# Splitting the last two gated tiles of a Conformer module by token halves, and adding up its layer-norm sums on other engines than TensorE

## The chip, the cores and the metric

The kernel runs on one core of a Trainium2 chip. A core has five engines that work at the same time, each through its own list of instructions in order: TensorE (PE, matrix products), VectorE (DVE), ScalarE (ACT), GpSimd (POOL), and SyncE (SP), whose list here holds nothing but DMA issues. The metric is the device time of one execution in microseconds (us), as the median of the runs shown. Times inside the program are us from the start of one profiled execution.

## The reference, cut to what matters

Two layers over 512 tokens and 1024 channels. Layer 0 is a hybrid of state-space heads and attention with a SwiGLU feed-forward; layer 1 is a Conformer convolution module with another SwiGLU; a final RMS norm closes. The change lies inside the Conformer module:

```python
def conformer_conv(h, w1, b1, w_dw, b_dw, ln_g, ln_b, w2, b2):
    a, gt = jnp.split(h @ w1 + b1, 2, axis=-1)      # first pointwise layer, 1024 -> 2 x 1024
    u = a * jax.nn.sigmoid(gt)                      # gate
    u = causal_depthwise_conv(u, w_dw, b_dw)        # 31 taps along the tokens, per channel
    u = jax.nn.silu(layer_norm(u, ln_g, ln_b))      # mean and variance over the 1024 channels
    return u @ w2 + b2                              # second pointwise layer
```

The norm needs all channels of a token before any of them goes on. The convolution is causal: an output token needs itself and the 30 tokens before it.

## The kernel before, in words

Channels lie on the 128 partitions and tokens along the free dimension, so the 1024 channels are 8 tiles, numbered k = 0 to 7, of 128 x 512. `CUTS` holds the two halves of the tokens, `H0` (0 to 255) and `H1` (256 to 511).

A product of exact 32-bit quality is made of three matmuls on rounded parts: weights and activations are split into a high part (`hi`, a cast on ACT, L208) and a low part (`lo`, a subtraction, L209, on DVE or POOL), and `products` (L212 to 225) adds hi*hi (L221), hi*lo (L222) and lo*hi (L224) over 8 contraction tiles: 24 matmuls an output tile. `slab` (L195) loads 1 MB of weights into one of two `raw` buffers by an SP DMA (L200), and fills one of two `whi` and one of two `wlo` buffers; each is free again when its last reader is done.

Stages of the Conformer module, for each k:

- **Products** `pa` and `pg` (`a` and the gate) for 512 tokens, 48 matmuls, into the two banks with the tag `pj`.
- **Gate**: sigmoid on ACT (L992), `u = (pa + b) * sigmoid` on DVE (L996) into `cu`, with zeros ahead of the first token.
- **Shifted copies** (`shifted`, L962): 16 SP DMAs (L967) copy `cu` into `u4[k]` (in the profile: `u`), which holds each group of 32 channels four times, shifted by 0 to 3 tokens, so that a matmul of 32 output channels covers four taps.
- **Convolution** (`conv`, L969): 32 matmuls (8 steps of 4 taps, times 4 channel groups, into `cps`, L975) with filters `w4[k]` that POOL builds (L930); ACT evicts each half into `cv[k, half]` (L979). The profile counts two instructions for one of these 32-bit matmuls; products with rounded parts count one.
- **Layer norm** (`layer_norm(c)`, L1006) by halves of the tokens: 8 matmuls with a matrix of 1/1024 (`mu`, L1011) give the mean on all partitions, DVE subtracts it (L1015), ACT squares (L1019), 16 matmuls against ones give the variance (`var`, L1021), DVE takes the inverse root in 12 small steps, two matmuls spread it (`lnr`, L288), DVE multiplies (L1028), ACT applies silu (L1029) and rounds to `ch` (L1030), and DVE makes the low part `cl` (L1031).
- **Second pointwise layer** (`pw2(c)`, L1035): 8 output tiles `pq` for H0, then 8 for H1; DVE adds each to the residual `xT` (L608), whose squares feed the next norm.

The code is written with the convolution of tile k-2 behind the products of tile k, the first halves of 4 to 7 ahead, `layer_norm(H0)`, the second halves of 4 to 7, `layer_norm(H1)`, and then `pw2`. The order on every engine is not this one: a scheduler lays the instructions out when the program is built, by its own estimates of durations, and waits go by data and by buffers. So the order that stands in the built program is shown below where it matters.

## Time and profile before

| | us |
|---|---|
| median of 3 runs (lowest, highest) | 1847.52 (1847.27, 1849.47) |
| the profiled execution's own time | 1844.22 |
| its span, first to last instruction | 1842.5 |
| TensorE busy in the span | 1764.2 (96%) |
| DVE, ACT, POOL busy | 999.3, 740.7, 347.6 |
| mean granted TensorE clock | 0.983 |

The profile page gives the busy time of each engine, its rows by source line, and the chain of work that ended last. A row such as `L975 PE MATMUL cps<-u,w 128*32 128x256 f32 x512 | 31.9, 380 | 1.6` reads: line 975, TensorE, output `cps` from `u` and `w`, shapes, 512 instructions; 31.9 us busy and 380 ns on average; 1.6 us idle just before them, with what ended that idle time. Matmuls overlap in the array, so the pitch from one start to the next is shorter than one duration. In views by stretches of time (windows), a row gives the stretch, its length, each engine's busy time with its instructions, the granted clock, the share of the DMA engines and GB/s. In a timeline, a row gives start, duration and a count of merged instructions, with idle time before them in brackets.

The Conformer module runs from about 1256 us, where the third product tile starts, to 1460 us, where the second feed-forward starts.

### The profile page before, as it was taken

Reading aid. Unit: us, or ns where it says so; the run is one execution under the profiler, and the core shown is the slowest. Engines: PE = TensorE matmul, PEld = TensorE weight load, DVE = VectorE, ACT = ScalarE, POOL = GpSimd, SP = SyncE. Lnnn points to the kernel's source line nnn. Section 1 sums busy time; section 2 is a strip of 40 time slices with the busy share of each in tenths; the row PEclk is TensorE's granted clock in tenths of the full one; section 3 lists DMA queues with packets and bytes.
Section 4 is the critical chain, followed back from the end, with each engine's and each line's share of the span. In section 5 each row is a group of like instructions: output and inputs, shape, how many; then the busy total and the mean of one; then the engine's idle time right before and its main releaser. Section 6 shows DMA issues by size and latency. Waiting matters only on the chain.

```text
span 1842.5 us, 25006 instructions
## 1 busy us (share of the span) xinstructions
PE 1764.2 (96%) x9775; PEld 1438.8 (78%) x9775; DVE 999.3 (54%) x1944; ACT 740.7 (40%) x1473; POOL 347.6 (19%) x278
## 2 busy tenths in 40 slices
PE   5999999999999999977999999999999999999998
PEld 3777687788778787767888888897568988888887
DVE  7756657555655556658674673373204743333336
ACT  6465646455454444434222222252215532122235
POOL 0013314224542423432000000021121100000001
PEclk9999999999999999988999999999998999999999
DMA  9455544454545445343655562253640522323233
GB/s 309 125 143 152 154 119 125 111 150 138 133 131 149 127 157 142 104 128 115 228 187 179 183 206 81 87 177 78 178 122 24 161 92 92 92 92 114 70 97 132
DMA packets 233219, 247.85 MB, mean 135 GB/s; under 512 B 14074, under 2 KB 198204, under 8 KB 233101
## 3 DMA queue, kind: packets, MB, share of 16 engines
q1 hardware_dynamic: 223117, 208.50, 38.0%
q0 software_dynamic: 9984, 37.75, 6.2%
q8 instruction: 77, 1.26, 0.3%
q14 instruction: 41, 0.34, 0.1%
HBM read 228.73 MB, written 8.64 MB: 129 GB/s over the span
## 4 chain that ended last, share of the span: by engine, by line
PE 83%; DVE 6%; DMA 5%; ACT 2%; issue 1%; POOL 1%; SPq 0%; DVEq 0%; ACTq 0%; POOLq 0%
PE fd L221 4%; PE fd L222 4%; PE fd L224 4%; PE fg L222 4%; PE fu L221 4%; PE fg L221 4%; PE fu L222 4%; PE fu L224 4%; PE fg L224 4%; PE cps L975 3%; PE s L733 2%; DMA ar<-a_dram 2%; PE z L221 2%; PE z L222 2%; PE z L224 2%; PE qq L221 2%
## 5 line engine op out<-in xcount | busy, mean ns | idle before, releaser
L221 PE MATMUL fd<-uh,wd_h 128*128 128x512 f32 (+1 forms) x448 | 148.6, 347 | 0.9 <-DVE xT L608 0.9
L222 PE MATMUL fd<-uh,wd_l 128*128 128x512 f32 (+1 forms) x448 | 147.0, 344 | 0.0
L209 DVE TENSOR_TENSOR wf_l<-wf_w,wf_h 128x1024 fp32r<-128x1024 f32 x88 | 106.1, 1241 | 75.4 <-ACT wf_h L208 75.4
L208 ACT CAST wf_h<-wf_w 128x1024 fp32r<-128x1024 f32 x88 | 87.6, 1047 | 116.7 <-PE fd L224 71.9
L263 POOL TENSOR_TENSOR n_acc<-n_acc,n_q 128x256 f32<-128x256 f32 x32 | 30.2, 943 | 526.4 <-ACT n_q L259 526.3
L222 PE MATMUL fg<-n_h,wf_l 128*128 128x512 f32 x320 | 125.3, 391 | 1.0 <-DVE wf_l L209 1.0
L221 PE MATMUL fg<-n_h,wf_h 128*128 128x512 f32 x320 | 125.3, 392 | 0.5 <-ACT wf_h L208 0.5
L222 PE MATMUL fu<-n_h,wf_l 128*128 128x512 f32 x320 | 124.7, 390 | 0.0
L221 PE MATMUL fu<-n_h,wf_h 128*128 128x512 f32 x320 | 124.5, 389 | 0.0
L208 ACT CAST wd_h<-wd_w 128x1024 fp32r<-128x1024 f32 (+1 forms) x64 | 57.1, 940 | 101.3 <-PE fd L224 81.1
L759 ACT ACTIVATE s<-s,nm 128x128 f32<-128x128 f32 x192 | 79.5, 416 | 43.9 <-DVE nm L755 39.9
L885 DVE TENSOR_TENSOR fs<-fs,fu 128x512 f32<-128x512 f32 x40 | 27.5, 688 | 127.3 <-PE fu L224 127.3
L221 PEld LDWEIGHTS fd<-uh,wd_h 128*128 128x128 f32 x448 | 84.1, 188 | 11.9 <-DVE xT L608 1.3
L608 DVE SCALAR_TENSOR_TENSOR xT<-fd,mod,xT 128x512 f32<-128x512 f32 (+1 forms) x64 | 39.1, 615 | 98.3 <-PE fd L224 98.1
L222 PEld LDWEIGHTS fd<-uh,wd_l 128*128 128x128 f32 x448 | 84.2, 188 | 10.5
L224 PE MATMUL fd<-ul,wd_h 128*128 128x512 f32 (+1 forms) x448 | 91.9, 343 | 0.0
L209 DVE TENSOR_TENSOR wd_l<-wd_w,wd_h 128x1024 fp32r<-128x1024 f32 (+1 forms) x64 | 68.2, 1099 | 34.9 <-ACT wd_h L208 34.6
L162 DVE SCALAR_TENSOR_TENSOR adaa<-adaw,cs,adaa 128x512 f32<-128x512 f32 x112 | 85.0, 759 | 2.6
L884 ACT ACTIVATE fs<-fg 128x512 f32<-128x512 f32 x40 | 23.9, 598 | 146.7 <-PE fg L224 146.7
L224 PEld LDWEIGHTS fd<-ul,wd_h 128*128 128x128 f32 x448 | 72.9, 188 | 10.6
L186 POOL TENSOR_TENSOR adap<-adap 128x512 f32<-128x512 f32 (+2 forms) x72 | 79.1, 1099 | 5.0
L224 PE MATMUL fu<-n_l,wf_h 128*128 128x512 f32 x320 | 79.1, 389 | 0.0
(405 smaller groups left out, 4538.9 us busy)
## 6 DMA issues: line engine op xcount, KB each, us to landing
adaw<-in_ada_w POOLq DMA_DIRECT2D x24, 1024.0 KB, 5.7
wf_w<-in_ffn_w_gate SPq DMA_DIRECT2D x22, 1024.0 KB, 5.3
wf_w<-in_ffn_w_up SPq DMA_DIRECT2D x22, 1024.0 KB
wd_w<-in_ffn_w_down SPq DMA_DIRECT2D x16, 1024.0 KB, 5.2
adap<-in_ada_w POOLq DMA_DIRECT2D x24, 512.0 KB, 5.8
wd_w<-in_ffn_w_down SPq DMA_DIRECT2D x16, 768.0 KB, 4.3
wa_w<-in_hy_w_out SPq DMA_DIRECT2D x20, 512.0 KB, 6.8
u<-cu SPq DMA_DIRECT2D x128, 67.5 KB, 2.0
```

What stands on the lines that cost most here:

```text
L162: V.scalar_tensor_tensor(acc, ws[k // 4][:, k % 4, :], cs[:, k:k + 1], acc, op0=ALU.mult, op1=ALU.add)
L186: G.tensor_tensor(w[:, 0:n], w[:, 0:n], w[:, n:2 * n], op=ALU.add)
L208: S.copy(hi[:, s:e], raw[:, s:e])
L209: eng.tensor_tensor(lo[:, s:e], raw[:, s:e], hi[:, s:e].bitcast(F32), op=ALU.subtract)
L221: PE.matmul(ps[:, cols], hi[:, o(k):o(k) + P], xh, start=k == 0, stop=False)
L222: PE.matmul(ps[:, cols], lo[:, o(k):o(k) + P], xh, start=False, stop=False)
L224: PE.matmul(ps[:, cols], hi[:, o(k):o(k) + P], acts[k][1][:, cols], start=False, stop=k == nk - 1)
L263: (V if k >= self.n - 3 else G).tensor_tensor(self.acc, self.acc, sq, op=ALU.add)
L608: V.scalar_tensor_tensor(xT[m][:, cols], ps[:, cols], mod[l][:, go + m:go + m + 1], xT[m][:, cols], op0=ALU.mult, op1=ALU.add)
L733: marks[hp, 0] = marks[hp, 1] = PE.matmul(ps[:, o:o + 2 * wd].rearrange("p (e w) -> p e w", e=2), q, k, start=True, stop=True)
L759: S.activation(s[:, o:o + wd], s[:, o:o + wd], AF.Exp, bias=nm, accum_out=l)
L975: PE.matmul(ps[g * 32:(g + 1) * 32, :], w4[k][:, g * 8 + m, :], u4[k][:, g, t:t + w], start=m == 0, stop=m == 7)
```

## The change: what it does

**Halves.** For k = 6 and 7 the products, the gate and the shifted copies are made for H0 first. Their H1 halves come later in the code, behind `layer_norm(H0)`'s sums and ahead of the H1 convolutions. Each half has 48 matmuls of 256 columns, a sigmoid, a gate, and 16 DMAs (284 columns for H0, 256 for H1, where before there were 16 of 540 for both). For the H0 convolution to need no token of H1, the taps move by one place in their table: the zero tap is now the first instead of the last, and the pad ahead of the tokens is 31 instead of 30.

**Sums.** The sum over channels is built as the tiles come: `csum` adds k = 0 to 4 on POOL and 5 and 6 on DVE, for both halves of the tokens. The mean then takes two matmuls, one for `csum` and one for tile 7, where it took eight. The squares of tiles 0 to 5 are added pairwise on DVE (two adds of 512 columns, in a buffer of three, `cvq`), and the variance takes 8 matmuls where it took 16.

**Order in the code.** Rounding and low parts of the normed tiles (`parts`) are a function of their own; for H0 it stands behind the H1 products.

```diff
@@ taps moved by one place @@
-    V.memset(wcol[96:128, :, :, 7], 0.0)
+    V.memset(wcol[0:32, :, :, 0], 0.0)
...
-    PAD = TAPS - 1
+    PAD = TAPS
...
-        def shifted(k, u):
+        def shifted(k, u, cols=ALL):
-            u4[k] = conf.tile([P, 4, T + 28], F32, tag="u4", name=f"u4_{k}", bufs=5)
+            if cols.start == 0:
+                u4[k] = conf.tile([P, 4, T + 28], F32, tag="u4", name=f"u4_{k}", bufs=5)
+            lo, hi = cols.start and cols.start + 28, cols.stop + 28
             for sft in range(4):
                 for g in range(4):
-                    nc.sync.dma_start(u4[k][sft * 32:(sft + 1) * 32, g, :], u[g * 32:(g + 1) * 32, sft:sft + T + 28])
+                    nc.sync.dma_start(u4[k][sft * 32:(sft + 1) * 32, g, lo:hi], u[g * 32:(g + 1) * 32, sft + lo:sft + hi])
@@ conv @@
+                if k == 1:
+                    csum[c.start] = conf.tile([P, T // 2], F32, tag=f"csum{c.start}", name=f"csum{c.start}", bufs=1)
+                    G.tensor_tensor(csum[c.start], cv[0, c.start], o, op=ALU.add)
+                elif 1 < k < KT - 1:
+                    (G if k < 5 else V).tensor_tensor(csum[c.start], csum[c.start], o, op=ALU.add)
...
+        def gated(k, ps, c=ALL):
+            th = tmp.tile([P, T], F32, tag="st_sq", name=f"cth{k}_{c.start}")
+            S.activation(th[:, c], ps[1][:, c], AF.Sigmoid, bias=b1[:, 8 + k:9 + k])
...
+            V.scalar_tensor_tensor(us[k][:, PAD + c.start:PAD + c.stop], ps[0][:, c], b1[:, k:k + 1], th[:, c],
+                                   op0=ALU.add, op1=ALU.mult)
+            shifted(k, us[k], c)
+        def pair(ws, k, c=ALL):
+            return [products(w, [grid(256, k % 2)], h, f"p{m}{k}_{c.start}", cols=c)[0] for m, w in zip("ag", ws)]
...
+            for k in (2 * j, 2 * j + 1):
+                c = H0 if j == 3 else ALL
+                gated(k, banks[k] if banks else pair(ws, k, c), c)
@@ layer_norm @@
-            for i, k in enumerate(range(KT)):
-                PE.matmul(mb, meanw, cv[k, n], start=i == 0, stop=i == KT - 1)
+            PE.matmul(mb, meanw, csum[n], start=True, stop=False)
+            PE.matmul(mb, meanw, cv[KT - 1, n], start=False, stop=True)
...
-                for b in range(nb):
-                    PE.matmul(vp[:, b:b + 1], sq[:, b * P:(b + 1) * P], ones[:, 0:1], start=i == 0 and b == 0,
-                              stop=i == KT - 1 and b == nb - 1)
+                if k == 1:
+                    vacc = two
+                elif k in (3, 5):
+                    V.tensor_tensor(vacc, vacc, two, op=ALU.add)
+            for i, sq in enumerate((vacc, two)):
+                for b in range(2 * nb):
+                    PE.matmul(vp[:, b % nb:b % nb + 1], sq[:, b * P:(b + 1) * P], ones[:, 0:1], start=i == 0 and b == 0,
+                              stop=i == 1 and b == 2 * nb - 1)
...
@@ the end of the module @@
         layer_norm(H0)
+        for k in (6, 7):
+            gated(k, pair(ws, k, H1), H1)
+        ...
+        parts(H0)
         for k in (4, 5, 6, 7):
             conv(k, CUTS[1:])
...
         layer_norm(H1)
+        parts(H1)
```

The rows that follow are the order in the built programs, one row for one instruction or a run of equal ones (the number behind the x counts them). A number in a name is the tile's k where it is small (`u_6`, `u_7`; `cps_0`, `mu`, `pa_0` stand for H0 or both halves, `cps_256`, `pa_256` for H1).

On SP, from the shifted copies of tile 5 on, before the change:

```order
L967 DMA u_5_10825<-cu_10821 32x540 x16
L200 DMA wq_1_w<-in_cv_w_pw 128x8x256
L967 DMA u_6_10953<-cu_10949 32x540 x16
L200 DMA wq_2_w<-in_cv_w_pw 128x8x256
L967 DMA u_7_11061<-cu_11057 32x540 x16
L200 DMA wq_3_w<-in_cv_w_pw 128x8x256
```

and with the change:

```order
L969 DMA u_5_10825<-cu_10822 32x540 x16
L200 DMA wq_1_w<-in_cv_w_pw 128x8x256
L969 DMA u_6_10954<-cu_10951 32x284 x16
L969 DMA u_7_11062<-cu_11059 32x284 x16
L969 DMA u_6_10954<-cu_10951 32x256 x16
L969 DMA u_7_11062<-cu_11059 32x256 x16
L200 DMA wq_2_w<-in_cv_w_pw 128x8x256
```

Tiles 6 and 7 take 64 issues in four groups instead of 32 in two, and the third weight slab of the second layer, `wq_2`, moves from between the groups to behind all of them.

On TensorE, from the H0 convolution of tile 7 (`cps_0` from `u_7`) to the end of the first half's variance, before the change, where `mu` is the mean and `var` the variance of H0:

```order
L975 MATMUL cps_0_11166<-u_7_11061,w_7_10879 32x256 x29
L975 MATMUL cps_256_11370<-u_6_10953,w_6_10767 32x256 x22
L1011 MATMUL mu_11201<-cv_0_11199,meanw 128x256
L975 MATMUL cps_256_11335<-u_5_10825,w_5_10639 32x256 x23
L1021 MATMUL var_11210<-ones,cvq_0_11212 128x1 x4
L1021 MATMUL var_11210<-ones,cvq_0_11221 128x1 x4
L975 MATMUL cps_256_11335<-u_5_10825,w_5_10639 32x256 x9
```

and with the change, from the same convolution (the rows of the H1 products of tile 7, 24 for `pa_256` and 24 for `pg_256`, are cut to the first of each):

```order
L977 MATMUL cps_0_11153<-u_7_11062,w_7_10881 32x256 x29
L221 MATMUL pa_256_0_11328<-n_h_9995,wp_3_h 128x256
...
L1019 MATMUL mu_11188<-cv_0_11186,meanw 128x256
L221 MATMUL pg_256_0_11353<-n_h_9995,wp_3_h 128x256
...
L977 MATMUL cps_256_11429<-u_4_10712,w_4_10524 32x256 x23
L977 MATMUL cps_256_11465<-u_5_10825,w_5_10639 32x256 x8
L1034 MATMUL var_11191<-ones,cvq_0_11193 128x1 x4
L977 MATMUL cps_256_11465<-u_5_10825,w_5_10639 32x256 x6
L1034 MATMUL var_11191<-ones,cvq_0_11210 128x1 x4
L977 MATMUL cps_256_11465<-u_5_10825,w_5_10639 32x256 x18
L977 MATMUL cps_256_11501<-u_6_10954,w_6_10768 32x256 x24
```

The H1 products of tile 7 now stand between its H0 convolution and the variance, and the H1 convolutions of tiles 4 and 5, which stood ahead of and beside the variance before, stand behind those products. Then come the spread of the norm, the rest of tile 6, the whole of tile 7's H1 convolution (32 matmuls), and `pq`.

On DVE with the change, around the gate of tile 7's H1 half (`cu` from `pa_256`):

```order
L1024 TENSOR_TENSOR cv_0_11150<-cv_0_11150,mu_11188 128x256
L1024 TENSOR_TENSOR cv_0_11186<-cv_0_11186,mu_11188 128x256
L1031 TENSOR_TENSOR cvq_0_11193<-cvq_0_11193,cvq_0_11198 128x512
L1031 TENSOR_TENSOR cvq_0_11193<-cvq_0_11193,cvq_0_11204 128x512
L996 SCALAR_TENSOR_TENSOR cu_11059<-pa_256_0_11328,pb,cth_256_11378 128x256
L1037 TENSOR_SCALAR lnv_11222<-var_11191 128x2
```

where before, the gate of tile 7 was a single instruction ahead of the whole norm:

```order
L996 SCALAR_TENSOR_TENSOR cu_10949<-pa_0_10897,pb,cth_10947 128x512
L996 SCALAR_TENSOR_TENSOR cu_11057<-pa_0_11005,pb,cth_11055 128x512
L1015 TENSOR_TENSOR cv_0_10523<-cv_0_10523,mu_11201 128x256
L1015 TENSOR_TENSOR cv_0_10635<-cv_0_10635,mu_11201 128x256
L1015 TENSOR_TENSOR cv_0_10763<-cv_0_10763,mu_11201 128x256
```

The gate that starts the last 16 copies is now queued behind the first half's eight subtractions and the two adds of squares. On ACT its sigmoid stands likewise behind the first six squares. From the first product of the second feed-forward to the end, the order on TensorE is the same in both programs.

More of the change, by code (lines that the diff above doesn't have):

```diff
@@ L983, in trunk_kernel @@
             banks = first_banks(ws, h, "p", nxt.cuts) if j == 0 else None
[L984 to L1000 removed]
+            for k in (2 * j, 2 * j + 1):
+                c = H0 if j == 3 else ALL
+                gated(k, banks[k] if banks else pair(ws, k, c), c)
+                if j:
+                    conv(k - 2, CUTS if j < 3 else CUTS[:1])
+                    if j < 3:
                         filters(k + 2)
[L1003 to L1004 removed]
         def layer_norm(c):
@@ L1029, in layer_norm, with parts @@
                 S.activation(t, t, AF.Silu, bias=lnb[:, k:k + 1], scale=lng[:, k:k + 1])
+        def parts(c):
+            for k in range(KT):
+                t = cv[k, c.start]
                 S.copy(ch[k][:, c], t)
@@ L1045, in trunk_kernel @@
         layer_norm(H0)
+        for k in (6, 7):
+            gated(k, pair(ws, k, H1), H1)
+        ch = [hpool.tile([P, T], F32R, tag="hh", name=f"ch{k}") for k in range(KT)]
+        cl = [hpool.tile([P, T], F32R, tag="hl", name=f"cl{k}") for k in range(KT)]
+        parts(H0)
         for k in (4, 5, 6, 7):
```

39 lines of the change are left out of this document (12 added, 27 removed).

## The prediction

> **What bounds the kernel now.** I read the page's busy times first, then the Conformer module by stretches, then what TensorE waited for there, then its timeline. On the page:
>
> ```profile
> span 1842.5 us, 25006 instructions
> PE 1764.2 (96%) x9775; PEld 1438.8 (78%) x9775; DVE 999.3 (54%) x1944; ACT 740.7 (40%) x1473; POOL 347.6 (19%) x278
> ```
>
> TensorE sets the end, so a matmul taken out is worth its pitch, and a wait filled is worth its length. What the change touches lies between the first product of tile 6 and the end of the second pointwise layer, 1330.95 to 1459.95. Four stretches: products of 6 and 7; H1 convolutions and the first norm; `pq` of H0; `pq` of H1 (columns: stretch, length, busy PE, PEld, DVE, ACT, POOL with counts, granted clock, DMA share, GB/s):
>
> ```profile
> 1330.95:1356.75 25.80, 25.80 (x165) 19.84 (x161) 0.75 (x1) 4.01 (x6) 6.12 (x3) 1.00 0.41 109
> 1356.75:1399.05 42.30, 39.98 (x517) 24.89 (x516) 7.81 (x29) 11.44 (x23) 5.28 (x3) 1.00 0.28 77
> 1399.05:1435.53 36.48, 33.28 (x230) 32.14 (x230) 23.87 (x60) 23.58 (x54) 12.86 (x8) 0.86 0.18 58
> 1435.53:1459.95 24.42, 24.42 (x205) 24.42 (x205) 18.43 (x38) 12.94 (x22) 4.77 (x4) 1.00 0.56 176
> ```
>
> The last two hold the same `pq` products, yet the third is 12 us longer than the fourth. What TensorE waited for in the 129.0 us:
>
> ```profile
> PE pq L221 <- ACT ch L1030: 2.4, 4, 0.7
> PE cps L975 <- DMA u<-cu: 1.6, 1, 1.6
> PE pq L221 <- DVE xT L608: 1.3, 1, 1.3
> PE pq L222 <- POOL wq_l L209: 0.3, 1, 0.3
> ```
>
> Only 5.6 us. The third stretch also has the lower clock. Finer stretches of TensorE alone:
>
> ```profile
> 1398.35:1403.50 5.15, 2.79 (x17) 1.00 0.00 0
> 1403.50:1405.97 2.47, 2.47 (x24) 0.99 0.00 0
> 1405.97:1416.20 10.23, 10.23 (x50) 0.50 0.01 2
> 1416.20:1421.80 5.60, 5.60 (x48) 1.00 0.00 0
> ```
>
> For 5.15 us TensorE was about half idle, waiting for the first half's rounded tiles one by one; 2.5 us later the clock stood at half for 10.2 us.
>
> **Removed: six of eight mean matmuls a half, and half of the variance.** The timeline's start times give the pitch (columns: start, duration, what, count):
>
> ```profile
> 1394.18 2.43 PE L1011 MATMUL mu<-cv,meanw 128*128 128x256 f32 x10
> 1396.44 0.61 PE L288 MATMUL lnr_b<-lnr_d,ones 128*128 128x128 f32 x4
> 1383.72 1.95 PE L1021 MATMUL var<-ones,cvq 128*128 128x1 f32 x16
> 1385.59 1.70 PE L975 MATMUL cps<-u,w 128*32 128x256 f32 x23
> ```
>
> Ten `mu` instructions take 1396.44 - 1394.18 = 2.26, so 0.226 each; 16 `var` take 1.87, so 0.117. The groups by line have 32 `mu` and 64 `var`:
>
> ```profile
> L1011 PE MATMUL mu<-cv,meanw 128*128 128x256 f32 x32 | 8.4, 395 | 0.0
> L1021 PE MATMUL var<-ones,cvq 128*128 128x1 f32 x64 | 9.5, 270 | 0.0
> ```
>
> Left are 8 and 32: **-24 x 0.226 = -5.4** and **-32 x 0.117 = -3.7**. The sums move to POOL and DVE, which the second row of the stretches shows at 5.28 and 7.81 of 42.3 us. POOL's subtractions of the same kind, on 1024 columns:
>
> ```profile
> 1416.40 4.77 POOL L209 TENSOR_TENSOR wq_l<-wq_w,wq_h 128x1024 fp32r<-128x1024 f32 x2 [53.10 <-ACT wq_h L208]
> ```
>
> That is 2.4 us each, so about 0.6 for a `csum` add of 256 columns. All of them run beside products and convolutions of later tiles; were that cover gone, the mean would wait for one, 0.6 us.
>
> **Split: 96 matmuls of 512 columns become 192 of 256.** Starts of the products of 6 and 7 with what follows, and of two neighbouring half products:
>
> ```profile
> 1330.95 0.50 PE L221 MATMUL pa<-n_h,wp_h 128*128 128x512 f32 x1
> 1342.06 3.66 PE L975 MATMUL cps<-u,w 128*32 128x256 f32 x64
> 1345.65 0.50 PE L221 MATMUL pa<-n_h,wp_h 128*128 128x512 f32 x1
> 1356.75 11.00 PE L975 MATMUL cps<-u,w 128*32 128x256 f32 x200
> 1445.11 0.28 PE L221 MATMUL pq<-ch,wq_h 128*128 128x256 f32 x1
> 1447.99 0.28 PE L221 MATMUL pq<-ch,wq_h 128*128 128x256 f32 x1
> ```
>
> Whole: 11.11 + 11.10 = 22.2. Halves: 8 x 2.88 = 23.0. **+0.8.** By the Trainium skill's "TensorE: Matmul & The Clock Gate", section "Back-to-back issue gap", 256 columns take 262 cycles and 512 take 518, so two halves would cost 1% more and the term 0.3; the pitches here, 0.120 and 0.231, say 4%, and I go by them. The convolutions are the same 8 x 3.59 us (1345.65 - 1342.06).
>
> **Moved: the last half's gate, copies and convolution.** SP issues the copies one after another:
>
> ```profile
> 1336.74 0.53 SPq L200 DMA_DIRECT2D wq_w<-in_cv_w_pw  x1
> 1343.66 10.94 SPq L967 DMA_DIRECT2D u<-cu  x16
> 1357.32 0.37 SPq L200 DMA_DIRECT2D wq_w<-in_cv_w_pw  x1
> 1358.36 11.33 SPq L967 DMA_DIRECT2D u<-cu  x16
> ```
>
> A 1 MB slab takes 0.37 to 0.53 us to issue and a 67.5 KB copy takes 11/16 = 0.69, so I take the cost as one of the issue and not of the bytes: a group of 16 halves costs 11 us too. (If it went by bytes, 5.5; that end shortens the waits below.) Four groups are 44 us of SP, and the last group must be ready for the last convolution. The convolution waited for the last of the groups above like this:
>
> ```profile
> 1369.37 0.59 PE L975 MATMUL cps<-u,w 128*32 128x256 f32 x2 [1.62 <-DMA u<-cu]
> ```
>
> so its first matmul can run 1369.37 - 1358.36 = 11.0 us after a group's first issue, and the other three channel groups up to 1.9 us later. What comes between the products' end and that issue:
>
> ```profile
> 1356.86 0.69 ACT L992 ACTIVATE cth<-pg,pb 128x512 f32<-128x512 f32 x1 [3.44 <-PE pg L224]
> 1357.58 0.75 DVE L996 SCALAR_TENSOR_TENSOR cu<-pa,pb,cth 128x512 f32<-128x512 f32 x1 [13.94 <-ACT cth L992]
> 1381.10 2.74 DVE L1015 TENSOR_TENSOR cv<-cv,mu 128x256 f32<-128x256 f32 x8 [22.77 <-PE mu L1011]
> 1432.31 2.35 DVE L209 TENSOR_TENSOR wq_l<-wq_w,wq_h 128x1024 fp32r<-128x1024 f32 x2
> ```
>
> 1.6 us for 512 columns; 1.2 for 256 is an estimate between that and its half. Now the path, in this execution's times. Tile 6 H0: products end 1330.95 + 5.76 = 1336.7, group one starts at 1337.9, its convolution may start at 1348.9; TensorE is there at 1336.7 + 3.6 + 5.8 + 3.6 = 1349.7. No wait. Group two starts when SP is free, 1348.9, so tile 7's H0 convolution may start at 1359.9; TensorE comes at 1349.7 + 3.6 + 5.8 = 1359.1: 0.8 us of wait, and the rows between fill the other channel groups. With those (nine matmuls of tile 4's H1, half the mean) it is 1365; H1's last products with the mean end near 1371.5. **The gate of the last half** is queued on DVE behind the eight subtractions (2.74 us) and two adds of 512 columns (0.6 each, half of a 1024-column `wq_l`). The mean stands after the first 24 products, at 1368.5, so the subtractions end at 1371.3, the adds at 1372.5 and the gate at 1373. Behind it on DVE wait the norm's small steps, needed only 10 us later; on SP `wq_2`, issued at 1384, with 22 us until its product, where such a slab takes 5.3 to land:
>
> ```profile
> wf_w<-in_ffn_w_gate SPq DMA_DIRECT2D x22, 1024.0 KB, 5.3
> ```
>
> Group three ends at 1372, so group four starts at 1373 and the last convolution has its channel groups from 1384.0 to 1385.9. TensorE arrives at 1371.5 + 2.6 + 3.6 + 1.9 + 3.6 + 0.5 = 1383.7, or 1385 with 0.3 us for each change between narrow and full matmuls (an estimate, under the 0.5 by which the lone pair at 1369.37 is longer than 2/64 of 3.66). Its other 28 matmuls (28/32 of 3.6) end at 1389; with 2 us for changes that I have not placed, `pq` starts near 1391, where before it started at 1399.05. **Waits on copies: 2.6 in place of 1.6, +1.0**; 0 to 7 are the bounds, zero if issues go by bytes, seven if SP or the queue ahead of the gate is 5 us later.
>
> **Filled: the start of `pq`.** Before, the first norm's tail came in one piece behind the last convolution, so that `pq` waited for `ch` four times, 2.4 us. Now the spread stands ahead of the last convolution, which is 3.6 us plus its wait: the eight multiplies (2.7 us) and most silus are done before `pq`. **-2.4** (0 if ACT lags by 5 us). With these half-idle 5 us goes the half clock: 50 instructions in 10.23 us, against 48 in 5.60 behind them, would take 5.8: **-4.4**.
>
> By the Trainium skill, same page, section "Why this matters for your kernels", the clock falls after idle gaps of about 3 us between bursts; the longest gap ahead of the fall here was 0.71 us. By that rule a wait of 2.6 us would never bring it back; by this trace half-idle stretches can, which is a rival below.
>
> **The second half's tail.** Its multiplies, silus and low parts must now fit under 27 us of `pq` H0 and not 36:
>
> ```profile
> 1418.32 2.74 DVE L1028 TENSOR_TENSOR cv<-cv,lnr_b 128x256 f32<-128x256 f32 x8 [2.52 <-PE lnr_b L288]
> 1428.49 3.90 DVE L1031 TENSOR_TENSOR cl<-cv,ch 128x256 fp32r<-128x256 f32 x3
> ```
>
> From the multiply to the last low part are 1432.4 - 1418.3 = 14.1 us, and `pq` H1 needs that part 5.5 us after it starts. With `pq` H0 from 1391, the variance (placed after 75 products, so 1401.5 to 1403.5), the root, and the spread (placed after 125) at 1410, H1 may start at 1410 + 14.1 - 5.5 = 1418.6; TensorE comes at 1391 + 27.5 = 1418.5. Even: I add **+0.6**, bounds 0 and 4.
>
> Sum: -5.4 - 3.7 + 0.8 + 1.0 - 2.4 - 4.4 + 0.6 = **-13.5**. From there on the order is the same, with TensorE at its pitch, so the gain arrives at the end. Against the profiled 1844.2 that is 1830.7; the median shown is 3.3 above that execution, so **1834.0**.
>
> **Rivals.**
> 1. *The half clock stays or comes back elsewhere.* For: the wait for the last copies comes in a stretch of narrow matmuls, with four of them in 2 us. Against: a wait of 1.6 us among such rows at 1369 left the clock at 1.00. It gives back 4.4: 1838.5. Chance 0.2.
> 2. *The second half's tail becomes the bound*, its low parts slowed beside POOL's `wq_l` (the three above took 1.30 us each). Against: those 14.1 us are already in the sum. Four us at the start of `pq` H1: 1838. Chance 0.13.
> 3. *SP is the bound*: an extra 4 to 5 us on group four, and the clock with it, -13.5 + 4.5 + 4.4: 1843. Chance 0.1.
> 4. *Slower: issues stretch when the queue is full.* The longest of 128 issues is three times the median:
>
> ```profile
> L967 SPq DMA_DIRECT2D u<-cu x128: 507/589/1681, 1255.5 to 1369.1; - x128
> ```
>
> If all 16 of group four went at 1.68 us, it would take 27 and not 11: -13.5 + 16 = +2.5, 1850. It decides from 0.84 us more an issue, 13.5/16. Against: 16 issues took 10.9 and 11.3 in the two groups above. Chance 0.05.
> 5. *It does not do what it says*: the split groups are there but all gains are eaten by switching, 1847. Chance 0.03.
>
> **Numbers.** The forecast has 0.49, with a range of its own of 1830 to 1837.5 from its bounds. Taking in the first three rivals gives 1829 to 1843.5. What a measurement tells from no change is 0.2%, 3.7 us: faster 0.87, same 0.07, slower 0.06.
>
> **What would show it.** Right: 8 `mu` and 32 `var` instructions; four groups of 16 copies of 11 us back to back on SP; a wait of `cps` for `u` of 1 to 3 us just ahead of `pq`; `pq` from about 1391 and 27 us for H0, at a clock of 1.00. Wrong: groups near 5.5 us (cost goes by bytes); clock 0.5 after 1385; a wait of `pq` for `cl` or `ch` at H1 of over 2 us; or the gain lost behind 1445 in waits for weights.

## The result, and the profile after

The change is faster: a median of 1833.79 us (1826.68 to 1844.15, 9 runs) against 1847.52 (1844.30 to 1849.47, 9 runs of the kernel before beside it), a ratio of 0.9922 with a 95% interval of 0.9903 to 0.9941. That is 13.7 us, nearly four times the 3.7 us that the prediction takes as the least that a measurement here tells from no change. The prediction was 1834.0 us, range 1829.0 to 1843.5.

The profiled execution of the change took 1834.18 us. Its page begins:

```profile
span 1832.4 us, 25139 instructions
PE 1755.0 (96%) x9815; PEld 1434.6 (78%) x9815; DVE 1006.2 (55%) x1946; ACT 740.0 (40%) x1475; POOL 356.2 (19%) x286
```

TensorE still fills 96% of the span, and is busy for 9.2 us less. The rest is read in one **stretch**, from the first product of tile 6 to the first product of the second feed-forward layer: 129.0 us before (1330.95 to 1459.95). After, by windows of the same four parts as in the prediction, and as a whole (columns: stretch, length, busy PE, PEld, DVE, ACT, POOL, granted clock, DMA share, GB/s):

```profile
1336.30:1377.51 41.21, 41.21 (x474) 33.32 (x470) 5.04 (x13) 7.34 (x16) 6.10 (x5) 1.00 0.31 81
1377.51:1397.08 19.57, 19.45 (x259) 11.18 (x259) 12.07 (x29) 10.00 (x21) 8.93 (x5) 0.91 0.32 92
1397.08:1424.82 27.74, 26.77 (x218) 26.31 (x218) 18.67 (x51) 20.68 (x47) 13.07 (x8) 1.00 0.35 112
1424.82:1449.89 25.07, 24.61 (x206) 24.41 (x205) 20.30 (x44) 13.69 (x26) 4.47 (x4) 1.00 0.55 171
...
1336.30:1449.89 113.59, 112.04 (x1153) 95.22 (x1150) 56.09 (x137) 51.72 (x105) 32.57 (x21) 0.98 0.37 110
```

129.0 became 113.6: **15.4 us less**. The third row matters most: `pq` of H0 took 27.74 us at clock 1.00, where it took 36.48 at 0.86. Behind the stretch nothing changed: from there to the end of the span are 1842.5 - 1459.95 = 382.5 us before and 1832.4 - 1449.89 = 382.5 after. Ahead of it this execution came to tile 6 5.35 us later than the one before. That shift is there already at the first feed-forward layer (856.31 and 861.56), ahead of anything that the change touches, and in the 14 profiled executions of this study tile 6 starts anywhere from 1325.9 to 1337.7 us; so the 10.1 us between the two spans are 15.4 less 5.35 that belong to the two executions. Subtract 5.35 to compare times of after with those of the prediction.

What TensorE waited for in the stretch (5.6 us in four rows before):

```profile
PE pq L221 <- DVE xT L608: 1.4, 2, 1.0
```

No wait for copies (`u`), none for `ch`. The matmuls of the sums, by groups in the same stretch (instructions | busy, mean ns | idle before):

```profile
L1034 PE MATMUL var<-ones,cvq 128*128 128x1 f32 x32 | 3.9, 249 | 0.1
L1018 PE MATMUL mu<-csum,meanw 128*128 128x256 f32 x4 | 1.3, 405 | 0.0
L1019 PE MATMUL mu<-cv,meanw 128*128 128x256 f32 x4 | 1.2, 379 | 0.0
```

32 and 8, where 64 and 32 stood. SP's timeline, in three pieces (the first group, the fourth, and all four):

```profile
1343.37 10.50 SPq L969 DMA_DIRECT2D u<-cu  x16
...
1381.65 10.51 SPq L969 DMA_DIRECT2D u<-cu  x16
...
1343.37 48.80 SPq L969 DMA_DIRECT2D u<-cu  x64
```

16 copies of half the columns take 10.5 us, as 16 whole ones took 10.9 and 11.3: the cost goes by issue. Four groups of 10.5 are 42 of the 48.8 us, so SP stood idle for about 6.8 and was not the bound. Last, the clock, in windows of TensorE alone and the rows of its timeline there:

```profile
1380.80:1384.20 3.40, 3.28 (x34) 1.00 0.11 25
1384.20:1387.60 3.40, 3.40 (x33) 0.51 0.22 52
1387.60:1391.00 3.40, 3.40 (x58) 0.99 0.21 52
```

```profile
1381.29 1.05 PE L1034 MATMUL var<-ones,cvq 128*128 128x1 f32 x8
1382.27 1.06 PE L977 MATMUL cps<-u,w 128*32 128x256 f32 x12
1383.26 1.05 PE L1034 MATMUL var<-ones,cvq 128*128 128x1 f32 x8
1384.24 6.61 PE L977 MATMUL cps<-u,w 128*32 128x256 f32 x84
...
1392.16 4.99 PE L977 MATMUL cps<-u,w 128*32 128x256 f32 x78
1397.08 0.39 PE L221 MATMUL pq<-ch,wq_h 128*128 128x256 f32 x1
```

The 10.2 us of half clock at the start of `pq` are gone, but 3.4 us are new, behind the 16 variance instructions (8 float32 matmuls) of the first half.

### The profile page after: what moved, and what is told of

Read it like the earlier page. It is cut to its first block, busy times and chain, and to the rows that moved or that the text cites. A ratio compares the mean times of both kernels' runs of the same rounds, so it can differ in the third digit from the quotient of the medians.

```text
span 1832.4 us, 25139 instructions
## 1 busy us (share of the span) xinstructions
PE 1755.0 (96%) x9815; PEld 1434.6 (78%) x9815; DVE 1006.2 (55%) x1946; ACT 740.0 (40%) x1475; POOL 356.2 (19%) x286
## 4 chain that ended last, share of the span: by engine, by line
PE 83%; DVE 6%; DMA 5%; ACT 3%; issue 1%; POOL 1%; SPq 0%; DVEq 0%; ACTq 0%
PE fd L221 4%; PE fd L222 4%; PE fd L224 4%; PE fg L222 4%; PE fg L221 4%; PE fu L222 4%; PE fu L221 4%; PE fu L224 4%; PE fg L224 4%; PE cps L977 3%; PE s L733 2%; DMA ar<-a_dram 2%; PE z L221 2%; PE z L222 2%; PE z L224 2%
## 5 line engine op out<-in xcount | busy, mean ns | idle before, releaser
L885 DVE TENSOR_TENSOR fs<-fs,fu 128x512 f32<-128x512 f32 x40 | 27.5, 688 | 127.3 <-PE fu L224 127.3
L222 PEld LDWEIGHTS fd<-uh,wd_l 128*128 128x128 f32 x448 | 84.2, 188 | 10.5
```

What stands on the lines that cost most here:

```text
L222: PE.matmul(ps[:, cols], lo[:, o(k):o(k) + P], xh, start=False, stop=False)
```

## The experiments

Every kernel was timed beside the kernel before on the same chip. The medians scatter by execution, in the profiled ones for the most part ahead of the stretch, so the table also gives the stretch of each profiled execution, what the view of waits lists for TensorE in it, and the half clock in it. *Rest* is the stretch less the waits and less half of the half clock: an estimate of TensorE's work at full clock.

| kernel | stretch | waits | half clock | rest | median | ratio (95%) |
|---|---|---|---|---|---|---|
| before | 129.0 | 5.6 | 10.2 | 118.3 | 1846.9 to 1850.0 | 1 |
| change | 113.6 | 1.4 | 3.4 | 110.5 | 1833.8 | 0.9922 (0.9903, 0.9941) |
| e1: sums only | 124.2 | 9.6 | 14.4 | 107.4 | 1842.0 | 0.9970 (0.9947, 0.9994) |
| e2: halves only | 139.0 | 7.3 | 17.1 | 123.2 | 1860.3 | 1.0087 (1.0054, 1.0120) |
| e5: halves, mean off | 130.1 | 6.9 | 17.1 | 114.7 | 1848.4 | 0.9991 (0.9975, 1.0007) |
| e6: halves, variance off | 126.5 | 5.6 | 3.4 | 119.2 | 1844.3 | 0.9977 (0.9962, 0.9991) |
| e9: before + fill | 123.9 | 3.5 | 0 | 120.4 | 1842.0 | 0.9961 (0.9945, 0.9978) |
| e10: sums only + fill | 120.5 | 4.5 | 0 | 116.0 | 1833.4 | 0.9913 (0.9883, 0.9943) |
| e11: change + unused sums | 121.8 | 0 | 10.2 | 116.7 | 1842.6 | 0.9956 (0.9935, 0.9976) |
| e4: last copies doubled | 124.5 | 6.7 | 10.2 | 112.7 | 1842.0 | 0.9972 (0.9949, 0.9995) |
| e3: 4 variance matmuls | 116.6 | 7.0 | 0 | 109.6 | 1833.8 | 0.9943 (0.9921, 0.9965) |
| e7: e3, gate first | 121.3 | 6.5 | 13.6 | 108.0 | 1836.4 | 0.9932 (0.9905, 0.9959) |
| e12: split on DVE | 113.8 | 3.9 | 0 | 109.9 | 1832.0 | 0.9898 (0.9867, 0.9928) |
| e8: tile 7 only | 117.4 | 4.3 | 3.4 | 111.4 | 1838.4 | 0.9935 (0.9912, 0.9958) |

Median less stretch lies between 712.9 and 721.3 us, so a difference of well over 8 us cannot lie wholly outside the stretch; a smaller one is read from the stretch of one execution and is as sure as that. The kernel before took 1846.9 to 1850.0 us beside the others, so ratios compare better than medians. The granted clock of whole executions, over all timed runs, bears the clock column out: its mean is 0.9856 in the change (9 runs) and 0.9821 to 0.9832 in the kernel before (74 runs beside the experiments), which is 4.4 to 6.4 us of 1840 (an estimate), where the stretch has 3.4.

### e1 and e2: one part of the change at a time

e1 is the kernel before with, in essence, these lines alone, e2 the change without them:

```diff
+                if k == 1:
...
+                    G.tensor_tensor(csum[c.start], cv[0, c.start], o, op=ALU.add)
+                elif 1 < k < KT - 1:
+                    (G if k < 5 else V).tensor_tensor(csum[c.start], csum[c.start], o, op=ALU.add)
...
+            PE.matmul(mb, meanw, csum[n], start=True, stop=False)
+            PE.matmul(mb, meanw, cv[KT - 1, n], start=False, stop=True)
...
+                elif k in (3, 5):
+                    V.tensor_tensor(vacc, vacc, two, op=ALU.add)
```

> The kernel before with the sums off TensorE alone (the csum adds, two mean matmuls a half, the squares added in pairs), tiles 6 and 7 whole. Theory (the terms of the sum are independent): the removed matmuls are worth -9.1 us, the half clock near the start of pq and the waits on ch stay: about 1838.4 us, ratio 0.995. Rival (the first norm's chain sets the start of pq in this order): only what is removed behind that start counts at once, and the 3.6 us removed ahead of it turn into waits for the root and the rounded tiles: -4.5 to -5.5 us, 1842 to 1843, ratio 0.997 or above.

> The change with the sums put back on TensorE: tiles 6 and 7 in halves, but eight mean matmuls and sixteen variance matmuls a half. Theory (terms independent): +0.8 +1.0 -2.4 -4.4 +0.6 = -4.4 us, 1843.1 us, ratio 0.9976; the 10.2 us of half clock near 1406 are gone. Rival (the two parts need each other, the halves free nothing without the sums): 0 or slower, ratio 1.000 or above, with a half clock among the variance matmuls.

Measured: e1 is worth 4.8 us in the stretch, about half the price of its matmuls, as its rival said; e2 is *slower* by 10.0 us. Together they are worth 15.4. The terms are not independent. In e1 the first norm stands where it stood, so what is taken away ahead of `pq` comes back as a wait (waits, then the timeline of TensorE at that place):

```profile
PE pq L221 <- ACT ch L1040: 4.9, 1, 4.9
PE pq L221 <- DVE xT L608: 1.9, 2, 1.2
```

```profile
1390.89 0.61 PE L288 MATMUL lnr_b<-lnr_d,ones 128*128 128x128 f32 x4
1396.41 0.58 PE L221 MATMUL pq<-ch,wq_h 128*128 128x256 f32 x1 [4.91 <-ACT ch L1040]
```

The wait for `ch` went from 2.4 to 4.9 us, and the half clock behind it from 10.2 to 13.7 (the 14.4 of the table hold 0.8 us of a later one, which runs on past the end of the stretch). By the table, in sum: rest -10.9, waits +4.0, clock +2.1, which is -4.8.

### e5 and e6: which of the two sums do the halves need?

e5 is the change with the old variance, e6 the change with the old mean.

> The change with the variance back on TensorE (sixteen matmuls a half), the mean alone taken off it. From the first product of tile 6 to the first product of the second feed-forward layer the kernel before took 129.0 us, the change 113.6, the change with both sums on TensorE 139.1, with two stretches of half clock (17 us). Theory (the eight mean matmuls are what made the halves slow: they wait for evictions one by one and delay the first norm): near the change plus the 3.7 us of variance matmuls, 116 to 120 us in that stretch, ratio 0.993 to 0.996. Rival (the variance in sixteen pieces, with its waits, holds the first norm up): 130 to 139 us, ratio 1.002 to 1.008.

> The change with the mean back on TensorE (eight matmuls a half), the variance alone in pair sums. Theory (the mean is what made the halves slow): 130 to 136 us in the stretch from the first product of tile 6 to the second feed-forward layer, ratio 1.001 to 1.006, with half clock in it. Rival (the variance did it): the change plus the 5.4 us of mean matmuls, 118 to 120 us, ratio 0.994 to 0.996.

Neither theory held (e5 just reaches the 130 us of its rival, but not its ratio): putting the variance back costs 16.5 us for 3.7 us of matmuls, the mean 12.9 for 5.4. For e5 (and e2) ACT's timeline around the start of `pq` shows one reason:

```profile
1388.66 1.28 ACT L1037 ACT_TABLE_LOAD   x1
1389.96 1.09 ACT L1037 ACTIVATE cv<-cv,pb 128x256 f32<-128x256 f32 x2
1390.96 0.39 ACT L1042 CAST ch<-cv 128x256 fp32r<-128x256 f32 x1
1391.25 1.09 ACT L1037 ACTIVATE cv<-cv,pb 128x256 f32<-128x256 f32 x2
1392.36 1.28 ACT L992 ACT_TABLE_LOAD   x1
1393.65 0.47 ACT L992 ACTIVATE cth<-pg,pb 128x256 f32<-128x256 f32 x1
```

With sixteen variance matmuls a half, the scheduler sets tile 7's H1 products *behind* the variance. Its sigmoid (`cth`) then falls among the norm's silus, and ACT changes its function table three times in the stretch, at 1.28 us each, where the change does it once. `pq` stood for 4.2 us, and the clock fell for 10.2:

```profile
1394.18 0.58 PE L221 MATMUL pq<-ch,wq_h 128*128 128x256 f32 x1 [4.25 <-ACT cth L992]
```

So e2 is a different order as well as more matmuls; the halves could not be tried without the sums in the order of the change. For e5 the account closes: against the change 5.5 us of waits, 6.8 of clock and 4.2 of rest. e6 has one table load and 3.4 us of half clock; its waits are 4.2 us above the change's, and its rest is 8.7 above, 3.3 more than the mean's 5.4. e2, which has the same eight mean matmuls, has a rest 3.6 us above what both sums explain. Part of this is the price of changing between the convolution, whose matmuls fill 32 columns (`128*32` in the rows), and the others. In e2, one pair of its instructions set alone:

```profile
1373.96 0.62 PE L977 MATMUL cps<-u,w 128*32 128x256 f32 x2
1374.51 0.61 PE L1024 MATMUL var<-ones,cvq 128*128 128x1 f32 x4
```

From start to next start this pair takes 0.55 us, where a pair inside a long run takes 0.11 (64 in 3.59). In the timelines of the stretch, TensorE turns to the convolution 10 times in the change, 19 times in e2 and 14 times in e6. At 0.44 us a time, nine more are 4.0 us, enough for the 3.6 of e2, and four more are 1.8 of the 3.3 of e6 (estimates). The other 1.5 us of e6 were not found.

### e9 and e10: filling the wait with work that nobody needs

e9 adds to the kernel before, behind the first rounded tile; e10 adds to e1, behind the spread:

```diff
+                if k == 0 and c is H0:
...
+                    for i in range(20):
+                        PE.matmul(fill, ch[0][:, 0:P], ch[0][:, c], start=i == 0, stop=i == 19)
@@ e10 @@
+        if name == "lnr0":
...
+            for i in range(20):
+                PE.matmul(fill, ones, dg.rearrange("p b q -> p (b q)"), start=i == 0, stop=i == 19)
```

> The kernel before with 20 more matmuls that compute nothing that is used: products of the first rounded tile of the first half with itself, set just ahead of pq, where TensorE was about half idle for 5 us. At 0.115 us they are 2.3 us of work. Theory (the half clock of 10.2 us at 1406 comes from the half-idle stretch ahead of it): the clock stays at 1.00, 4.4 us come back, and the matmuls lie in waits of 2.4 us: 124.5 to 127 us in the stretch and not 129.0, ratio 0.9975 to 0.999. Rival (the clock does not hang on these waits): 129 to 131.5 us, half clock as before, ratio 1.000 to 1.0015.

> The sums off TensorE with tiles 6 and 7 whole, plus 20 float32 matmuls of 256 columns that compute nothing that is used, behind the spread of the first norm. Without them that kernel took 124.2 us from the first product of tile 6 to the second feed-forward layer, with one wait of 4.9 us for the first rounded tile and 13.7 us of half clock behind it. Theory (that wait costs twice, itself and the clock): the 20 matmuls at 0.23 us fill 4.6 us of the wait, the clock stays at 1.00, 6.8 us come back: 116.5 to 119 us, ratio 0.992 to 0.995. Rival (the halves are needed to gain more than the sums): 122 to 126 us, ratio 0.996 to 0.998.

Measured: e9 does 2.5 us more work and is 5.1 us faster in the stretch (the median by 0.39%). By groups and by windows (the second row: TensorE's busy time alone, `pq` of H0 from the end of the fill):

```profile
L1034 PE MATMUL fill<-ch 128*128 128x256 f32 x20 | 2.6, 287 | 0.7 <-ACT ch L1030 0.7
```

```profile
1402.40:1434.20 31.80, 29.91 (x249) 1.00 0.30 95
...
1329.11:1452.98 123.87, 120.39 (x1133) 98.97 (x1130) 52.25 (x127) 51.67 (x103) 29.10 (x17) 1.00 0.35 101
```

The clock is 1.00 throughout: 5.1 us less by the clock, 2.1 less of waits, 2.1 more of rest. Over all timed runs the mean granted clock of whole executions is 0.9858 in e9 (12 runs) and 0.9821 in the kernel before beside it (29 runs): 6.8 us of 1840 (an estimate), nearly all of the 7.3 us between the medians. So the half clock of the kernel before hung on the waits ahead of `pq`, and cost about 5 us. But waits are not the whole of it. In each trace the changes of the clock lie whole multiples of 3.41 us apart; of the last two such windows ahead of the fall, the emptier one kept the clock (the windows are cut to within 0.1 us; columns as in the first windows above):

```profile
1399.05:1402.56 3.51, 2.21 (x12) 1.60 (x12) 3.51 (x12) 3.51 (x9) 0.00 (x0) 1.00 0.00 0
1402.56:1405.97 3.41, 3.05 (x26) 3.05 (x27) 2.78 (x8) 3.41 (x13) 0.00 (x0) 0.99 0.00 0
```

The second, behind which it fell, holds 16 variance instructions of one column (`128x1` in the rows) and 10 of `pq`; in e9 two windows there hold 16 of them and 14 of `pq` each, and the clock stays (more on this in the last section). e9 also bears on the rule that the prediction weighed (the Trainium skill, "TensorE: Matmul & The Clock Gate", section "Why this matters for your kernels": gaps of over about 3 us between bursts): no single wait ahead of `pq` in the kernel before was longer than 0.71 us, and yet filling them brought the full clock back; the measurement decides.

In e10 a float32 matmul shows as two instructions, so 20 of them are 40 and took 8.5 us, not the 4.6 that I had expected:

```profile
1386.35 8.80 PE L292 MATMUL fill<-lnr_d,ones 128*128 128x256 f32 x40
1394.80 0.47 PE L221 MATMUL pq<-ch,wq_h 128*128 128x256 f32 x1
```

The fill is about 3.6 us too long (`pq` starts 65.6 us after tile 6's first product, in e1 62.0), and the kernel still gains 3.7 us in the stretch, with no half clock in it. Its median lies 8.6 us below e1's, and its ratio 0.0057, more than the stretch explains; with 5 runs, the remainder stays open. The clock over all runs agrees with the stretch: its mean is 0.9862 here (5 runs) and 0.9817 in e1 (12 runs), 8.3 us of 1840 (an estimate), where the stretch has 7.2. So much of what the halves bring can be had without them: e1's disadvantage against the change is all in its waits and its clock, since its rest, 107.4, is below the change's 110.5. With some 11 matmuls instead of 20 it should lie about 3.6 us lower (an estimate from the two starts of `pq`); that was not run.

### e11: the removed matmuls put back where nobody waits for them

```diff
+            for i in range(6):
+                PE.matmul(fm, meanw, cv[KT - 1, n], start=i == 0, stop=i == 5)
...
+            for b in range(4 * nb):
+                PE.matmul(fv[:, b % nb:b % nb + 1], two[:, b % 4 * P:(b % 4 + 1) * P], ones[:, 0:1], start=b == 0, stop=b == 4 * nb - 1)
```

> The change with the matmuls put back on TensorE that it took away, 12 of the mean and 32 of the variance, but writing to banks that nobody reads, so that no wait hangs on them. Theory (a matmul is worth its pitch whatever it computes): +9.1 us in the stretch from the first product of tile 6 to the second feed-forward layer, 121 to 123.5 us against 113.6, ratio 0.996 to 0.998. Rival (in the change the sums mattered by the chain of waits that they shorten, and TensorE has room): 113.5 to 118 us, ratio 0.992 to 0.994. Had the kernel with both sums on TensorE and the halves been slow by matmuls alone, it would be at 139.

(The 32 of the variance are the profile's instructions, 16 matmuls.) Measured: 121.8 us, 8.2 more than the change, and not one wait. By windows, the whole stretch, and two places where single-column matmuls stand together:

```profile
1337.30:1459.09 121.79, 121.79 (x1210) 105.44 (x1206) 62.12 (x137) 52.17 (x105) 31.69 (x21) 0.96 0.34 103
```

```profile
1412.42:1415.83 3.41, 3.41 (x34) 1.00 0.01 2
1415.84:1419.25 3.41, 3.41 (x18) 0.50 0.17 25
```

In the changed structure TensorE is the bound, and the matmuls count: the total is the theory's, not the rival's. What it is made of is not, since 6.8 us more of half clock (3.4) and 1.4 us fewer waits are in the 8.2; by the rest alone it is 6.2. From each start to the next in the trace, the added matmuls take 9.7 us, or 8.4 at full clock, near their price; the convolutions and `pq` take 2.3 us less at full clock than in the change, for which TensorE's 8 turns to the convolution in place of 10 give only a part. The second fence: in 3.41 us TensorE was never idle, but 32 of its 34 instructions belong to matmuls of one column, and the clock fell right behind.

### e3 and e7: fewer variance matmuls

e3 adds the last pair of squares on DVE as well, and four matmuls a half are left; e7 is e3 with the H1 gates written ahead of the first norm.

```diff
-                elif k in (3, 5):
+                elif k in (3, 5, 7):
@@ e7 @@
+        for k in (6, 7):
+            gated(k, pair(ws, k, H1), H1)
         layer_norm(H0)
-        for k in (6, 7):
-            gated(k, pair(ws, k, H1), H1)
```

> The change with the last pair of squares added on DVE as well, so that the variance takes four matmuls a half and not eight. Theory: 16 matmuls x 0.117 = -1.9 us against the change, and without the cluster of variance matmuls near 1380 the 3.4 us of half clock at 1384 do not come: another -1.7; 1830 to 1832 us, ratio 0.990 to 0.991. Rival (the adds beside POOL's weight split set the gate of the last half): one more add of 1.8 us ahead of the gate delays group four of the copies and the last convolution; 0 to +2 us against the change, ratio 0.992 to 0.993, with a wait of cps for u of 1 to 3 us.

> The run with four variance matmuls a half, with the gates of the second halves of tiles 6 and 7 written ahead of the first norm instead of behind it. That run took 116.7 us in the stretch, with waits of 2.0 us of the last convolution for its copies and 3.5 us of pq for banks that DVE had not yet emptied. Theory (the adds ahead of the gate delay the copies): the wait for copies goes, 2 us less, 114 to 115 us, ratio 0.990 to 0.992. Rival (DVE is now the engine that decides): the wait moves to pq for ch, xT or cl, 117 to 120 us, ratio 0.993 to 0.996.

Measured: in e3 the half clock is gone from the stretch, as expected, but waits of 7.0 us take its place, and in sum it is no better than the change. Its waits:

```profile
PE pq L221 <- DVE xT L608: 3.5, 4, 2.4
PE cps L977 <- DMA u<-cu: 2.0, 1, 2.0
```

The first is DVE, which empties `pq`'s banks late; the second is the late gate, as the rival had it. e7 loses the wait for copies and gets others, 2.4 us of the variance for its squares and 2.7 of the spread for the root, and 13.6 us of half clock: DVE decides, as the rival had it, but at other places than the rival named. The intervals of both overlap that of the change, so neither is shown to differ from it.

### e4: how much room does the last group of copies have?

```diff
+                    cut = (lo, (lo + hi) // 2, hi) if k == 7 and lo else (lo, hi)
+                    for x, y in zip(cut, cut[1:]):
+                        nc.sync.dma_start(u4[k][sft * 32:(sft + 1) * 32, g, x:y], u[g * 32:(g + 1) * 32, sft + x:sft + y])
```

> The change with the copies of tile 7's second half issued in 32 pieces of half the columns, so that SP needs 10 to 11 us more for group four if the cost goes by issue. The planner then sets the last convolution among the first pq products. Theory (the second half's tail has no slack, as forecast): mean and variance of the second half come 8 to 10 us later, and pq of H1 waits that long for cl or ch: +7 to +10 us against the change, 1841 to 1844, ratio 0.9965 to 0.998. Rival (SP and the second half's tail have room): 0 to +2 us, 1834 to 1836, ratio 0.992 to 0.9935. If the cost goes by bytes, group four stays at 11 us and nothing moves.

Measured: 10.9 us more in the stretch and 0.5% more in the ratio, the theory's figure, but only in part for its reason. SP now works without a pause, and `pq` waits for rounded tiles:

```profile
1336.82 59.27 SPq L971 DMA_DIRECT2D u<-cu  x80
```

```profile
PE pq L221 <- ACT ch L1049: 5.6, 4, 2.6
```

The timeline has the places, the first and the last of the four:

```profile
1388.13 0.38 PE L221 MATMUL pq<-ch,wq_h 128*128 128x256 f32 x1 [1.37 <-ACT ch L1049]
...
1429.33 0.58 PE L221 MATMUL pq<-ch,wq_h 128*128 128x256 f32 x1 [2.64 <-ACT ch L1049]
```

Three of them, 3.0 us, stand at the start of `pq` of H0, which in this order no longer has the last convolution ahead of it; only the last, 2.6 us, is the second half's tail. With 1.1 us of another wait, less the change's 1.4, the waits make 5.3 of the 10.9 us; 3.4 are clock and 2.2 rest. Again, what was doubled is the number of issues, not of bytes. So the second half's chain did run out of room, but as the order changed too, the run does not show how much room there was.

### e12: the weight splits moved from POOL to DVE

```diff
-                         G if c is H0 else V)
+                         V)
```

> The change with the weight splits of the second pointwise layer's first half on DVE and not on POOL. Theory (the two adds of 512 columns ahead of the last gate took 1.8 us each and not 0.6 because POOL was splitting weights meanwhile): with POOL quiet they take 0.5 to 0.7 us each; TensorE had no wait there, so the stretch stays at 112 to 115.5 us, ratio 0.991 to 0.993. Rival (the adds are slow of themselves): 1.5 us or more each, and DVE with 10 us more work makes pq wait: 116 to 120 us, ratio 0.994 to 0.996.

Measured: the four adds of 512 columns take 0.68 us each (first row, by groups). In the change the two ahead of the gate took 3.63 together, the tile's view says 0.83 and 2.70 (second fence):

```profile
L1031 DVE TENSOR_TENSOR cvq<-cvq,cvq 128x512 f32<-128x512 f32 x4 | 2.7, 682 | 0.0
```

```profile
L1031 DVE TENSOR_TENSOR cvq<-cvq,cvq x2: 834/1766/2697, 1377.6 to 1378.5; 128x512 f32<-128x512 f32 x2
```

POOL's timeline of the change at that place:

```profile
1375.46 10.30 POOL L209 TENSOR_TENSOR wq_l<-wq_w,wq_h 128x1024 fp32r<-128x1024 f32 x4 [28.13 <-ACT wq_h L208]
```

So POOL's splitting was the cause of the slow adds. By the Trainium skill's "SBUF — State Buffer", section "Who interferes with whom", a DVE instruction with two SBUF inputs and a POOL one that reads SBUF contend for a shared port, which the first holds for its whole instruction while the other stands still; the 2.0 us by which the slower add is longer than 0.68 fit inside one of POOL's subtractions (four in 10.30 us), so the trace agrees. The stretch is as long as the change's, 113.8 us, with no half clock and a wait of 2.5 us for copies in exchange. Its median is the lowest of all, but with an interval that overlaps the change's it is not shown to be better.

### e8: tile 7 alone in halves

```diff
-                c = H0 if j == 3 else ALL
+                c = H0 if k == 7 else ALL
@@ ... @@
-        for k in (6, 7):
+        for k in (7,):
             gated(k, pair(ws, k, H1), H1)
```

> The change with tile 7 alone in halves and tile 6 whole, so that SP issues 16 copies fewer and TensorE has 48 matmuls of 512 columns in place of 96 of 256. Theory (the halves pay by the work that they set among the first norm's chain, and one tile's products are too little): less than 2 us of work stand behind the spread, pq waits 3 to 4 us for its rounded tiles and the clock falls to half for 7 to 10 us; 118 to 123 us, ratio 0.995 to 0.998. Rival (one tile is enough): 113 to 116 us with no half clock, ratio 0.991 to 0.993.

Measured: 117.4 us, between the two theories. The wait of `pq` for `ch` is 2.0 us and not 3 to 4, and the half clock 3.4:

```profile
PE pq L221 <- ACT ch L1047: 2.0, 3, 1.0
PE lnr_b L288 <- DVE lnr_d L285: 1.8, 1, 1.8
```

One tile brings most of the gain: 11.6 of 15.4 us.

## Why the prediction was right, step by step

The median came out 0.2 us from the forecast, which is luck beside its scatter. By the stretch, -15.4 us were measured where the sum said -13.5.

- **What bounds the kernel.** TensorE, with waits as the second item: right. In e11 no wait is left, and 28 matmuls that nobody waits for make the stretch 8.2 us longer.
- **The sums, -9.1.** The counts, 8 `mu` and 32 `var`, came as forecast. Rest before less rest after is 118.3 - 110.5 = 7.8, and the forecast for both sums and halves was 8.3 (9.1 - 0.8). Two misses nearly cancel in it: from each start to the next in the traces, at full clock and without waits, the mean and the variance take 10.3 us less and not 9.1, and the products of tiles 6 and 7 take 24.4 us where they took 22.2, so the split cost 2.2 and not 0.8. And the step "a matmul taken out is worth its pitch" holds only where no chain takes over: with tiles 6 and 7 whole (e1), half of it went into the wait for `ch`.
- **Waits on copies, +1.0.** Mis-sized: no wait at all. The groups took 10.5 us and not 11, and TensorE came later itself. The wait before (1.6) went too, so the waits on copies were worth -1.6.
- **The gate of the last half.** Forecast 1373; it ran at 1381.15, less 5.35: 1375.8. The step that failed is "two adds of 512 columns (0.6 each)": beside POOL they took 1.8 on average. Nothing came of it, because TensorE reached the last convolution late as well: its 64 instructions are the last of the 78 that start at 1392.16, so it starts near 1393.1, less 5.35 is 1387.7, where 1385 was forecast; 1.7 us of that is the new half clock.
- **The start of `pq`, -2.4.** Right: no wait for `ch`; start at 1397.08 - 5.35 = 1391.7, forecast 1391; and 27.74 us for H0, forecast 27.5. The start has luck in it: TensorE came to the last convolution 2.7 us late, and the 2 us of changes that the forecast adds behind that convolution did not come there.
- **The half clock, -4.4.** That the 10.2 us go when the start of `pq` is filled was right (e9); the sum was missing what the first rival said, that some of it comes back: 3.4 us at 1384.2, so 3.4 us were gained and not 4.4. It came not with the wait for copies, as that rival had it, but behind the variance matmuls, at 1378.9 in the prediction's time.
- **The second half's tail, +0.6.** No wait for `cl` or `ch` at H1, only 1.4 us for `xT` in both halves, where there were 1.3. The 0.6 did not come. That there is little room agrees with e4, where copies 10 us later brought a wait of 2.6 us at H1; how little is not shown.
- **The list of what would show it.** Counts, SP's groups, the start and length of `pq` and its clock were as listed; "back to back" was not, nor the wait of `cps` for `u`.
- **Rivals.** The second (the tail) and third (SP) did not come; e4, which makes SP later by some 10 us, cost 10.9, with a changed order in it. The fourth, issues stretched to 1.68 us, did not come: 16 took 10.5, 0.66 each. The fifth, switching, cost part of the 2.2 us of the split, and did not eat the gain.

By parts the 15.4 are: waits 5.6 - 1.4 = 4.2, clock 5.1 - 1.7 = 3.4, and rest 7.8.

What the prediction did not see is that its two halves depend on each other: it priced each edit from the old trace and added up. That was right for both together, since the path was followed through both, but as a price list, as the expectations of e1 and e2 took it, it was wrong by 4 us for the sums alone and by 14 for the halves alone, with the wrong sign there.

## What to carry to other kernels

Follow the path through all edits together, then ask of each edit alone what chain would take over; a matmul is worth its pitch only where no wait grows by it. A wait of TensorE is paid twice when the clock falls behind it, so look at the clock's windows beside the waits, and try filling a short wait with matmuls that nobody reads before restructuring (e9: 2.5 us of added work, 5.1 us gained). Count DMA issues, not bytes, on a queue of many small copies.

## What the runs showed of the hardware that was not expected

- The clock can fall behind a window of TensorE that is full by the profile but holds single-column matmuls: 34 instructions in 3.41 us without idle time, 32 of them of one column, then 0.50 for 3.4 us (e11). Their number does not decide alone. Of the windows of 3.41 us in the 14 stretches, cut on the grid of each trace's clock changes, 19 hold 16 or more single-column instructions, counted by their starts. The clock fell behind five of them, with at most 0.4 us idle: beside the single-column ones these hold at most 15 instructions of the convolution (12 in the change) or at most 10 of 256 columns on the whole array. It stayed behind the other 14, which hold at least 18 or at least 13. In e12, with the variance code of the change, 16 lay beside 22 of the convolution, and the clock stayed; whether other executions of the change lose the 3.4 us is not shown.
- Turning to the convolution and back costs TensorE time: a pair of its instructions set alone took 0.55 us to the next start, where a pair inside a long run takes 0.11 (e2).
- 16 copies between SBUF tiles cost SP 10.5 us at half the columns and 10.9 to 11.3 at all of them.
- A DVE add of two SBUF tiles of 512 columns took 0.68 us with POOL quiet and up to 2.70 beside POOL's subtractions.
- A sigmoid set among silus cost ACT two more table loads of 1.28 us, just where TensorE waited for ACT.
